# RMSNorm with SiLU: blocks of 512 rows with four rows per partition, and an order fixed by the program

## The chip, the cores and the metric

The kernel runs on one core of a Trainium2 chip. The metric is the device time of one execution in microseconds (us), and the kernel before is given by the median of three runs. One further execution was taken under the profiler; its time is given beside its span, which runs from the first to the last instruction that the trace holds.

The engines that do the work are ACT (ScalarE, activation functions), DVE (VectorE, elementwise work), POOL (GpSimd, here small arithmetic on one value per row) and SP (SyncE, which issues the transfers). TensorE isn't used. Transfers between memory (HBM) and the on-chip buffer (SBUF, 128 partitions) run on 16 DMA engines.

## The reference

The input x has 8 x 1024 = 8192 rows of 2048 float32 values, 67.1 MB; the output has the same shape. Each row is divided by its root mean square, scaled by a vector gamma, and passed through SiLU:

```
rms = sqrt(mean(x ** 2, axis=-1, keepdims=True) + eps)      # eps = 1e-5
out = gamma * x / rms
return out * (1 / (1 + exp(-out)))                          # float32
```

Every value is read once and written once, so the kernel moves 134 MB. A row needs all of its values for its mean before any of them can be scaled.

## The kernel before

The 8192 rows are cut into 64 tiles of 128 rows, one row per partition, so that a tile is 1 MB and each partition holds one run of 8 KB. A pool of 23 buffers (`BUFS`) holds the tiles. Every tile is worked on in place: it is loaded into a buffer, changed there, and stored from the same buffer.

Four functions make up the work on tile i:

- `load(i)` (line 41) issues the transfer of 1 MB from SP.
- `stats(i)` runs Square on ACT (line 59), with the sum of the squares of each row as a second output `ss`; the squares themselves go to a scratch tile `sq` that nobody reads. ACT's accumulator is fetched by a small instruction of its own, which the profile lists as ACTIVATION_READ_ACCUMULATOR. Then POOL computes `var = ss / 2048 + eps` (line 61) and `rstd = var ** -0.5` (line 64), on 128 partitions by one column.
- `scale(i)` multiplies on DVE (line 68): tile times `rstd` of the row times `g`, where `g` is gamma copied to all partitions by POOL at the start (line 47).
- `finish(i)` runs Silu on ACT (line 73), issues the store from SP (line 74), and then issues the load of tile i + 16 (`LEAD`).

The loop at the end calls `stats(i)`, `scale(i - 1)` and `finish(i - 2)`. That is the order of the text, and it isn't the order in which the engines work: the Tile framework takes the program as a set of instructions with dependencies, puts them into an order of its own for each engine, with its own estimate of their times, and adds the semaphores. The order that results is seen only in the timeline. ACT has two kinds of work for each tile, Square and Silu, and works its instructions off in the order in which they were put. Each engine is a queue in this sense: an instruction that waits holds up all that stand behind it.

All transfers are issued from SP and go through one queue (q1 in the profile), which works them off in their order.

Of the kernel before, what the change touches and what calls it, by code (L numbers as in the profile page):

```python
# [1 line left out]

# [4 lines left out]

ACT = mybir.ActivationFunctionType
ALU = mybir.AluOpType


@with_exitstack
def kernel(
    ctx: ExitStack,
    tc: tile.TileContext,
    x: bass.AP,
    gamma: bass.AP,
    eps: bass.AP,
    out: bass.AP,
):  # L20


    nc = tc.nc
    P = nc.NUM_PARTITIONS
    bf16 = mybir.dt.bfloat16
    f32 = mybir.dt.float32
    x2 = x.flatten_outer_dims()
    o2 = out.flatten_outer_dims()
    n, d = x2.shape
    ntiles = n // P  # L30
    BUFS, LEAD = 23, 16

    singles = ctx.enter_context(tc.tile_pool(name="singles", bufs=1))
    pool = ctx.enter_context(tc.tile_pool(name="pool", bufs=BUFS))
    small = ctx.enter_context(tc.tile_pool(name="small", bufs=8))

    xts = {}

    def load(i):
        xt = pool.tile([P, d], f32, name="xt")  # L40
        nc.sync.dma_start(out=xt, in_=x2[i * P:(i + 1) * P])
        xts[i] = xt

    grow = singles.tile([1, d], f32)
    nc.sync.dma_start(out=grow, in_=bass.AP(tensor=gamma.tensor, offset=gamma.offset, ap=[[d, 1], gamma.ap[0]]))
    g = singles.tile([P, d], f32)
    nc.gpsimd.partition_broadcast(g, grow)  # L47
    half = singles.tile([P, 1], f32)
    nc.gpsimd.memset(half, -0.5)  # L49
    sq = singles.tile([P, d], bf16)  # L50

    for i in range(LEAD):
        load(i)

    rstds = {}

    def stats(i):
        ss = small.tile([P, 1], f32, name="ss")
        nc.scalar.activation(out=sq, in_=xts[i], func=ACT.Square, accum_out=ss)  # L59
        var = small.tile([P, 1], f32, name="var")  # L60
        nc.gpsimd.tensor_scalar(out=var, in0=ss, scalar1=1.0 / d, scalar2=float(eps),  # L61
                                op0=ALU.mult, op1=ALU.add)
        rstd = small.tile([P, 1], f32, name="rstd")
        nc.gpsimd.tensor_tensor(out=rstd, in0=var, in1=half, op=ALU.pow)  # L64
        rstds[i] = rstd

    def scale(i):
        nc.vector.scalar_tensor_tensor(out=xts[i], in0=xts[i], scalar=rstds.pop(i), in1=g,  # L68
                                       op0=ALU.mult, op1=ALU.mult)

    def finish(i):
        xt = xts.pop(i)
        nc.scalar.activation(out=xt, in_=xt, func=ACT.Silu)  # L73
        nc.sync.dma_start(out=o2[i * P:(i + 1) * P], in_=xt)
        if i + LEAD < ntiles:
            load(i + LEAD)

    for i in range(ntiles + 2):
        if i < ntiles:
            stats(i)  # L80
        if 0 <= i - 1 < ntiles:
            scale(i - 1)
        if i >= 2:
            finish(i - 2)


# [1 line left out]
_INS = ['x', 'gamma', 'eps']  # L88
_OUTS = [((8, 1024, 2048), 'float32')]

_NUMBERS = {'eps': 9.999999747378752e-06}


# [26 lines left out]
```

## Time and profile before

| | |
|---|---|
| time, median of 3 runs | 413.59 us (413.02 to 413.94) |
| time of the profiled execution | 412.76 us |
| span of the profiled execution | 410.8 us |
| ACT busy | 244.6 us (60%) |
| DVE busy | 150.4 us (37%) |
| POOL busy | 60.1 us (15%) |
| moved | 134.28 MB, mean 327 GB/s over the span |

The page shows the span in 40 slices of 10.27 us; each digit is the busy share of a slice in tenths, so 9 means 90% or more. The row of a group reads: line, engine, operation, output <- inputs, shapes, count | busy us, mean ns of one | idle time of the engine just before these instructions and who ended that idle time. Idle time of an engine that doesn't set the end costs nothing. A row of the timeline reads: start, duration, engine, line, operation, count, and in brackets how long the engine had been idle before and what released it. A row of stretches gives, for each stretch, its length, the busy time and count of DVE, ACT and POOL, the clock, the busy share of the DMA engines and the rate in GB/s.

### The profile page before, as it was taken

What the parts mean: (1) busy time and instruction counts of PE and PEld (TensorE: products, weight loads), DVE (VectorE), ACT (ScalarE), POOL (GpSimd) and SP (SyncE); (2) the same over time, 40 slices, a digit from 0 to 9 for tenths busy, and PEclk for the clock granted to TensorE, in tenths of its full rate; (3) what the DMA queues carried; (4) which work ended last, traced back from release to release, by engine and by line L of the source; (5) the groups of instructions that cost most, each with busy time, mean ns of one, the idle gap of its engine ahead of it and who ended that gap; (6) DMA issues with size and microseconds to landing.
All of it is one profiled execution on the core that took longest, in us unless ns stands there. A gap on an engine that the chain in (4) does not pass through costs nothing.

```text
span 410.8 us, 895 instructions
## 1 busy us (share of the span) xinstructions
DVE 150.4 (37%) x64; ACT 244.6 (60%) x194; POOL 60.1 (15%) x134
## 2 busy tenths in 40 slices
DVE  0067666634242323324424233232424233242422
ACT  4549999984636465554763645556463645546462
POOL 1176212210010101010201010101001010101100
DMA  7999999999999999999999987887844242424334
GB/s 308 419 424 422 416 426 427 425 428 426 427 428 427 428 426 428 427 428 428 428 427 428 365 303 298 300 312 281 295 179 165 112 194 102 204 102 166 140 136 171
DMA packets 18440, 134.28 MB, mean 327 GB/s; under 512 B 2049, under 2 KB 2049, under 8 KB 2049
## 3 DMA queue, kind: packets, MB, share of 16 engines
q1 hardware_dynamic: 18434, 134.23, 80.0%
q14 instruction: 6, 0.05, 0.0%
HBM read 67.12 MB, written 67.11 MB: 327 GB/s over the span
## 4 chain that ended last, share of the span: by engine, by line
issue 76%; POOL 10%; DVE 1%; ACT 0%; POOLq 0%
POOL rstd L64 7%; POOL var L61 3%; DVE xt L68 1%; ACT xt L73 0%; POOLq L64 0%; POOLq L115 0%; ACT sq L59 0%
## 5 line engine op out<-in xcount | busy, mean ns | idle before, releaser
L68 DVE SCALAR_TENSOR_TENSOR xt<-xt,rstd,g 128x2048 f32<-128x2048 f32 x64 | 150.4, 2352 | 253.7 <-POOL rstd L64 252.9
L73 ACT ACTIVATE xt<-xt 128x2048 f32<-128x2048 f32 x64 | 121.7, 1905 | 155.1 <-DVE xt L68 154.0
L59 ACT ACTIVATE sq<-xt 128x2048 bf16<-128x2048 f32 x64 | 121.2, 1894 | 5.7 <-DMA xt<-in_x_dram 5.6
L61 POOL TENSOR_SCALAR var<-ss 128x1 f32<-128x1 f32 x64 | 20.4, 319 | 327.6 <-ACT sq L59 316.1
L64 POOL TENSOR_TENSOR rstd<-var,half 128x1 f32<-128x1 f32 x64 | 37.0, 579 | 5.4 <-POOL var L61 0.2
L59 ACT ACTIVATION_READ_ACCUMULATOR sq<-xt 128x1 f32 x64 | 11.9, 186 | 0.0
L47 POOL PARTITION_BROADCAST g<-grow x1 | 2.3, 2302 | 8.2 <-issue 8.2
L59 ACT ACT_TABLE_LOAD x1 | 1.3, 1283 | 0.7 <-PEq L101 0.7
L73 ACT ACT_TABLE_LOAD x1 | 1.3, 1283 | 0.0
L49 POOL MEMSET half<- 128x1 f32 x1 | 0.1, 99 | 0.3 <-POOLq L101 0.3
L101 POOL MEMSET const-float32-0.0<- 128x1 f32 x1 | 0.1, 98 | 0.2 <-issue 0.2
L101 POOL MEMSET const-bfloat16-1.0<- 128x1 bf16 x1 | 0.1, 101 | 0.0
L101 POOL MEMSET const-uint8-127<- 128x1 uint8 x1 | 0.1, 101 | 0.0
L101 POOL MEMSET const-float32-1.0<- 128x1 f32 x1 | 0.1, 99 | 0.0
## 6 DMA issues: line engine op xcount, KB each, us to landing
xt<-in_x_dram SPq DMA_DIRECT2D x64, 1024.0 KB, 19.6
out_dram<-xt SPq DMA_DIRECT2D x64, 1024.0 KB, 18.2
grow<-in_gamma_dram SPq DMA_DIRECT2D x1, 8.0 KB
```

Of the source, the lines that this page charges most:

```text
L47: nc.gpsimd.partition_broadcast(g, grow)
L49: nc.gpsimd.memset(half, -0.5)
L59: nc.scalar.activation(out=sq, in_=xts[i], func=ACT.Square, accum_out=ss)
L61: nc.gpsimd.tensor_scalar(out=var, in0=ss, scalar1=1.0 / d, scalar2=float(eps), op0=ALU.mult, op1=ALU.add)
L64: nc.gpsimd.tensor_tensor(out=rstd, in0=var, in1=half, op=ALU.pow)
L68: nc.vector.scalar_tensor_tensor(out=xts[i], in0=xts[i], scalar=rstds.pop(i), in1=g, op0=ALU.mult, op1=ALU.mult)
L73: nc.scalar.activation(out=xt, in_=xt, func=ACT.Silu)
L101: nc = _bacc.Bacc("TRN2", target_bir_lowering=False, num_devices=1)
```

## The change

The rows are cut into 16 blocks of 512 rows. Partition p of a block holds four consecutive rows (`J = 4`), which are one run of 32 KB in memory, so that a transfer is 4 MB. Six buffers of 32 KB per partition take the place of 23 of 8 KB, with four blocks loaded at the start (`LEAD = 4`). The first buffer taken from the pool holds gamma until POOL has copied it to all partitions.

The work on a row stays, with these differences:

- Of the four rows of a partition, three are squared and summed on ACT as before; the fourth is done on DVE by `tensor_tensor_reduce`, which multiplies the row by itself and sums. The unused squares go to two float32 tiles in PSUM, `junk_a` for ACT and `junk_v` for DVE, in place of the bf16 tile in SBUF.
- `ss`, `var` and `rstd` have four columns, so POOL runs two instructions per block of 512 rows.
- The multiply on DVE stays one row per partition at a time (four per block). Silu runs on two rows of each partition at once, 4096 elements, after the second and after the fourth multiply.
- The block is stored by one transfer, and the load of block b + 4 is issued after it.
- The body stands in `tc.manual_schedule()`: each engine gets its instructions in the order of the text. That order is `stats(b + 1)` ahead of `finish(b)`, so the Squares of the next block stand ahead of the Silus of this one on ACT, and the reduce of the next block ahead of the multiplies of this one on DVE.

```diff
-    ntiles = n // P
-    BUFS, LEAD = 23, 16
+    J = 4
+    BUFS, LEAD = 6, 4
+    nblk = n // (P * J)
+    xb = x2.rearrange("(b p j) d -> b p (j d)", p=P, j=J)
+    ob = o2.rearrange("(b p j) d -> b p (j d)", p=P, j=J)
...
-    small = ctx.enter_context(tc.tile_pool(name="small", bufs=8))
+    small = ctx.enter_context(tc.tile_pool(name="small", bufs=4))
+    psum = ctx.enter_context(tc.tile_pool(name="psum", bufs=1, space=bass.MemoryType.PSUM))
...
+    junk_a = psum.tile([P, d], f32, name="junk_a")
+    junk_v = psum.tile([P, d], f32, name="junk_v")
...
+    def load(b):
+        xt = pool.tile([P, J * d], f32, name="xt")
+        nc.sync.dma_start(out=xt, in_=xb[b])
+        blocks[b] = xt
...
+    def row(b, j):
+        return blocks[b][:, j * d:(j + 1) * d]
...
+    def stats(b):
+        ss = small.tile([P, J], f32, name="ss")
+        for j in range(J):
+            if j == J - 1:
+                nc.vector.tensor_tensor_reduce(
+                    out=junk_v, in0=row(b, j), in1=row(b, j), scale=1.0, scalar=0.0,
+                    op0=ALU.mult, op1=ALU.add, accum_out=ss[:, j:j + 1])
+            else:
+                nc.scalar.activation(out=junk_a, in_=row(b, j), func=ACT.Square,
+                                     accum_out=ss[:, j:j + 1])
+        var = small.tile([P, J], f32, name="var")
         nc.gpsimd.tensor_scalar(out=var, in0=ss, scalar1=1.0 / d, scalar2=float(eps),
                                 op0=ALU.mult, op1=ALU.add)
+        rstd = small.tile([P, J], f32, name="rstd")
         nc.gpsimd.tensor_tensor(out=rstd, in0=var, in1=half, op=ALU.pow)
+        rstds[b] = rstd
...
+    def finish(b):
+        for j in range(J):
+            nc.vector.scalar_tensor_tensor(out=row(b, j), in0=row(b, j), scalar=rstds[b][:, j:j + 1],
+                                           in1=g, op0=ALU.mult, op1=ALU.mult)
+            if j % 2:
+                pair = blocks[b][:, (j - 1) * d:(j + 1) * d]
+                nc.scalar.activation(out=pair, in_=pair, func=ACT.Silu)
+        nc.sync.dma_start(out=ob[b], in_=blocks.pop(b))
+        del rstds[b]
...
+    with tc.manual_schedule():
+        grow = pool.tile([P, J * d], f32, name="xt")
+        nc.sync.dma_start(out=grow[0:1, 0:d],
+                          in_=bass.AP(tensor=gamma.tensor, offset=gamma.offset, ap=[[d, 1], gamma.ap[0]]))
+        for b in range(LEAD):
+            load(b)
+        nc.gpsimd.memset(half, -0.5)
+        nc.gpsimd.partition_broadcast(g, grow[0:1, 0:d])
+        stats(0)
+        for b in range(nblk):
+            if b + 1 < nblk:
+                stats(b + 1)
+            finish(b)
+            if b + LEAD < nblk:
+                load(b + LEAD)
```

More of the change, by code (lines that the diff above doesn't have):

```diff
@@ L24 @@
     P = nc.NUM_PARTITIONS
-    bf16 = mybir.dt.bfloat16
     f32 = mybir.dt.float32
@@ L29 @@
     n, d = x2.shape
-    ntiles = n // P
-    BUFS, LEAD = 23, 16
+    J = 4
[3 more added lines that the diff above has]
+    ob = o2.rearrange("(b p j) d -> b p (j d)", p=P, j=J)
     singles = ctx.enter_context(tc.tile_pool(name="singles", bufs=1))
     pool = ctx.enter_context(tc.tile_pool(name="pool", bufs=BUFS))
-    small = ctx.enter_context(tc.tile_pool(name="small", bufs=8))
[L37 to L42, printed above, removed]
@@ L44 @@
-    grow = singles.tile([1, d], f32)
-    nc.sync.dma_start(out=grow, in_=bass.AP(tensor=gamma.tensor, offset=gamma.offset, ap=[[d, 1], gamma.ap[0]]))
-    g = singles.tile([P, d], f32)
[L47 to L60, printed above, removed]
+    small = ctx.enter_context(tc.tile_pool(name="small", bufs=4))
@@ new lines @@
+    psum = ctx.enter_context(tc.tile_pool(name="psum", bufs=1, space=bass.MemoryType.PSUM))
+    g = singles.tile([P, d], f32)
+    half = singles.tile([P, J], f32)
+    junk_a = psum.tile([P, d], f32, name="junk_a")
+    junk_v = psum.tile([P, d], f32, name="junk_v")
+    blocks, rstds = {}, {}
+    def load(b):
[4 more added lines that the diff above has]
+        return blocks[b][:, j * d:(j + 1) * d]
@@ L61, in stats @@
         nc.gpsimd.tensor_scalar(out=var, in0=ss, scalar1=1.0 / d, scalar2=float(eps),
                                 op0=ALU.mult, op1=ALU.add)
-        rstd = small.tile([P, 1], f32, name="rstd")
+        rstd = small.tile([P, J], f32, name="rstd")
         nc.gpsimd.tensor_tensor(out=rstd, in0=var, in1=half, op=ALU.pow)
[L65 to L84, printed above, removed]
+        rstds[b] = rstd
[8 more added lines that the diff above has]
+        del rstds[b]
```

## The prediction

> **What bounds the kernel now.** I read the page's busy times and slices first, then the groups, the timeline, the waits, and the stretches at both ends.
>
> ```profile
> span 410.8 us, 895 instructions
> DVE 150.4 (37%) x64; ACT 244.6 (60%) x194; POOL 60.1 (15%) x134
> ...
> DMA  7999999999999999999999987887844242424334
> GB/s 308 419 424 422 416 426 427 425 428 426 427 428 427 428 426 428 427 428 428 428 427 428 365 303 298 300 312 281 295 179 165 112 194 102 204 102 166 140 136 171
> ...
> q1 hardware_dynamic: 18434, 134.23, 80.0%
> ...
> HBM read 67.12 MB, written 67.11 MB: 327 GB/s over the span
> ```
>
> No engine is busy for more than 60% of the span, and the DMA runs full for 22 of 40 slices (some 226 us) and then falls to a third. So the transfers do not set the end, and neither does any engine's total work: an order does. The groups give the durations, the timeline the order:
>
> ```profile
> L68 DVE SCALAR_TENSOR_TENSOR xt<-xt,rstd,g 128x2048 f32<-128x2048 f32 x64 | 150.4, 2352 | 253.7 <-POOL rstd L64 252.9 <-DMA xt<-in_x_dram 0.8
> L73 ACT ACTIVATE xt<-xt 128x2048 f32<-128x2048 f32 x64 | 121.7, 1905 | 155.1 <-DVE xt L68 154.0 <-DMA out_dram<-xt 1.2
> L59 ACT ACTIVATE sq<-xt 128x2048 bf16<-128x2048 f32 x64 | 121.2, 1894 | 5.7 <-DMA xt<-in_x_dram 5.6
> L64 POOL TENSOR_TENSOR rstd<-var,half 128x1 f32<-128x1 f32 x64 | 37.0, 579 | 5.4 <-POOL var L61 0.2
> L61 POOL TENSOR_SCALAR var<-ss 128x1 f32<-128x1 f32 x64 | 20.4, 319 | 327.6 <-ACT sq L59 316.1 <-issue 11.2
> L59 ACT ACTIVATION_READ_ACCUMULATOR sq<-xt 128x1 f32 x64 | 11.9, 186 | 0.0
> ```
>
> ```profile
> 22.52 0.45 POOL L61 TENSOR_SCALAR var<-ss 128x1 f32<-128x1 f32 x2 [11.22 <-issue]
> ...
> 83.74 5.49 ACT L73 ACTIVATE xt<-xt 128x2048 f32<-128x2048 f32 x3
> ...
> 401.24 0.55 POOL L64 TENSOR_TENSOR rstd<-var,half 128x1 f32<-128x1 f32 x1
> 401.82 2.35 DVE L68 SCALAR_TENSOR_TENSOR xt<-xt,rstd,g 128x2048 f32<-128x2048 f32 x1 [4.78 <-POOL rstd L64]
> 404.20 1.91 ACT L73 ACTIVATE xt<-xt 128x2048 f32<-128x2048 f32 x1 [3.33 <-DVE xt L68]
> 406.14 0.33 SPq L74 DMA_DIRECT2D out_dram<-xt  x1
> ...
> 379.57 0.19 POOL L61 TENSOR_SCALAR var<-ss 128x1 f32<-128x1 f32 x1 [6.31 <-ACT sq L59]
> ...
> 386.70 0.19 POOL L61 TENSOR_SCALAR var<-ss 128x1 f32<-128x1 f32 x1 [6.31 <-ACT sq L59]
> ```
>
> At 83.74 us ACT runs three Silus in a row and has none in stock afterwards. From there ACT does Silu of a tile, Square of the next, and then waits 3.33 us: the next Silu needs the DVE multiply, which needs POOL's rstd, which needs that same Square. POOL's row returns every 7.13 us (379.57 to 386.70). That loop, 7.13 us a tile from about 84 us to the last Silu (some 45 tiles, 321 us), sets the end. The tiles themselves are there early: the Squares waited 5.6 us in all for loads. The transfers' own floor comes from a stretch in which they ran without a gap, loads and stores mixed:
>
> ```profile
> DMA packets 7031, 51.24 MB, mean 427 GB/s; under 512 B 777, under 2 KB 777, under 8 KB 777
> ```
>
> At 427 GB/s (60 to 180 us) the 134.28 MB would need 314.5 us.
>
> **The change part by part.**
>
> *Order.* In the new text ACT gets, per block of 512 rows, three Squares of the next block and two double Silus of this one; DVE one reduce of the next block, then four multiplies of this one. The multiplies of block b need only the statistics of b, finished a whole block earlier, so the loop goes. ACT per block: 3 x 1.90 us (Square and its accumulator read, which overlap slightly; the rows give 1.894 and 0.186) plus 2 x 3.66 us (5.49 us for three Silus, so 1.83 each) = 13.0 us. DVE: 4 x 2.352 = 9.4 us plus the reduce.
>
> *The reduce*, tensor_tensor_reduce, is in no row. Its bounds: 2.35 us (the multiply, also two inputs of 2048 elements in one pass) and 4.7 us (twice that, as for two passes). I take 2.35, the nearest row. DVE then has 11.8 us a block, at worst 14.1. *The double Silu* is bounded by 3.6 and 3.8 us (1.83 and 1.905 us twice); the Squares' target in PSUM I leave at 1.894 us. *POOL* gets tiles of four columns: 0.19 and 0.55 us at one column as the timeline has them, at most four times that (3.0 us), 16 times instead of 64. All of this lies under the transfers, because a block's load and store, 8.39 MB, take 19.6 us at 427 GB/s. Without that cover ACT would be the limit, 16 x 13.0 = 208 us, still less.
>
> *Transfers.* The bytes stay. 128 transfers of 1 MB become 32 of 4 MB, and runs of 8 KB become 32 KB; no row has such a size. To bound it:
>
> ```profile
> 1.00:3.00 2.00, 0.00 (x0) 1.00 (x1) 0.00 (x0) 1.00 0.37 66
> 3.00:6.10 3.10, 0.00 (x0) 0.01 (x1) 0.00 (x0) 1.00 0.97 402
> 6.10:42.00 35.90, 15.01 (x7) 24.86 (x21) 16.78 (x15) 1.00 1.01 422
> 406.10:407.00 0.90, 0.00 (x0) 0.01 (x1) 0.00 (x0) 1.00 0.15 64
> 407.00:409.40 2.40, 0.00 (x0) 0.00 (x0) 0.00 (x0) 1.00 1.00 413
> 409.40:410.80 1.40, 0.00 (x0) 0.00 (x0) 0.00 (x0) 1.00 0.01 0
> ...
> 236.00:300.00 64.00, 21.17 (x9) 34.05 (x28) 6.64 (x18) 1.00 0.82 294
> ```
>
> (columns after the stretch: its length, DVE, ACT, POOL, clock, DMA share, GB/s). A store alone on idle queues moved at 413 GB/s and 1 MB transfers in a full queue at 427: what belongs to a transfer rather than to its bytes is visible at some 3%. A quarter as many transfers and runs could save three quarters of as much again, 2.4%, so 437 GB/s at best; at worst the large runs do no better than the lone store, 413. I take 432, the middle of 427 and 437, since each engine still has eight runs and one small completion packet per transfer, but each run is four times as long: 134.28 / 0.432 = 310.8 us.
>
> The Trainium skill (DMA: Bandwidth & Descriptors, Where 436 GB/s comes from) puts the ceiling at 435.2 GB/s, 16 ports of 32 B at 850 MHz. As an estimate from that page the transfers would take 308.5 us, 2.3 less than my term; the 427 of this trace lies below the ceiling, as it must.
>
> *Queueing on SP.* One queue still carries gamma, four loads, then store b and load b+4 in turn. A load of block b+4 sits behind the store of b, which waits for the last double Silu of b. It also needs the buffer of b-2, whose store is two block times older. Before, eight transfers were in flight:
>
> ```profile
> xt<-in_x_dram SPq DMA_DIRECT2D x24, 1024.0 KB, 19.6
> ...
> SPq L74 <- ACT xt L73: 203.4, 34, 6.7
> SPq L41 <- DMA xt<-in_x_dram: 80.0, 40, 2.7
> SPq L74 <- DMA out_dram<-xt: 61.1, 29, 2.1
> ```
>
> 19.6 us to landing is eight times 2.45 us, and SP waited for older transfers 141 us in all. If that limit counts transfers, eight of 4 MB never bind; if bytes, two still bridge 19.4 us of queue. So SP's waits cost nothing as long as each store is issued before the queue runs dry. That I work out at the two ends, where least stands ahead of it.
>
> *Head.* First bytes by the rows above: by 6.1 us 1.38 MB had moved (2 x 66 + 3.1 x 402 kB), 3.3 us worth at 422, so the start costs 2.8 us. A block takes 9.7 us. Block 1 lands at 2.8 + 19.4 + 0.5 = 22.7; the reduce ends at 25.1 (POOL's first arithmetic came at 22.5 before, and is in time); four multiplies to 34.5, the last double Silu to 38.1, and 0.9 us more to the first byte of the store (406.14 to 407.0): 39.0. The four loads occupy the queue until 2.8 + 38.8 = 41.6. So there is 2.6 us of slack, 0.2 with the slow reduce.
>
> *Tail.* Load 15 is the 28th block to move and lands at 2.8 + 28 x 9.7 = 274.4, say 275. Stores 12 and 13 then still fill the queue until 294.4. Store 14 waits for the reduce of 15 and the multiplies of 14: 275 + 2.35 + 9.4 + 3.66 + 0.9 = 291.3. Store 15: 9.4 us later, 300.7, against 304.1. Slack 3.1 and 3.4 us, about 1 with the slow reduce. So I put the gaps at 0, at most 3 us.
>
> *Sum.* 2.8 start + 310.8 transfers + 0.5 (the four unmixed loads at 422 rather than 427) + 0.6 (four unmixed stores at the end, between 0 and the 1.3 us that 413 would cost) + 1.3 after the last byte (the last stretch above) = 316.0 us of span. The profiled execution took 412.76 us at a span of 410.8, so 2.0 us lie around it: 318.0. The median of the runs lay 0.8 above the profiled one, so 319.
>
> **The rivals.**
>
> *Turn-taking inside a block.* If a multiply on one row waits for the Silu on another row of the same buffer, DVE pauses 3.66 us between its second and third multiply. A block then takes DVE 15.4 us (19.1 if it pauses after the fourth too), still under 19.4; but head and tail lose their slack, 1.1 + 0.6 + 2.7 us: about 323. For it: one buffer now holds what four did. Against: the text addresses each row by its own columns.
>
> *The pinned order does not decouple.* If each block's statistics are waited for in its own turn, as now, a block costs 5.7 + 0.74 + 9.4 + 3.66 = 19.5 us, and 21.9 with the reduce in line; with 12.8 us until the first block lands and 11.9 us for the last store that is 337 to 375 of span, so 340 to 378. For it: that is exactly what the timeline shows now. Against: Squares of b+1 stand ahead of the Silus of b in the new text.
>
> *Slower: the large strides collide in memory.* Sixteen engines would walk addresses four times as far apart as now. If that costs transfer rate everywhere, the kernel is slower from 134.28 MB / (412.8 - 2.0 - 2.8 - 1.3 us) = 330 GB/s downwards. At the lowest sustained rate of a busy stretch here, 294 GB/s (236 to 300 us), it would take 456.7 + 6.1 = 463 us. Against it: a block stays one contiguous 4 MB piece, and the full slices hold 426 to 428 GB/s whatever addresses they pass; the 294 comes with stores issued one by one, not with full queues.
>
> For that rival the Trainium skill has a rule (the same page, Latency and other measured facts): row pitches at large powers of two slow copies, 207 GB/s each way at 512 KiB and 164 at 2 MiB against 214. Here the pitch goes from 8 to 32 KiB, below all of these, so by that rule little is lost; no run so far shows it.
>
> **How the numbers follow.** The forecast, transfers bound from end to end, gets 0.77; turn-taking 0.10; no decoupling 0.08; collision 0.05, of which 0.04 ends slower than before and 0.01 level. Low end: 437 GB/s without gaps, 307.3 + 4.6 + 2.8 = 314.7. High end: 413 GB/s with 3 us of gaps, 325.1 + 4.1 + 3 + 2.8 = 335. I give 313 to 336, which holds the forecast and turn-taking. The last two rivals lie outside. What a measurement of this kernel can tell from no change is about 0.2%: faster 0.95, same 0.01, slower 0.04.
>
> **What would show it.** Right: DMA slices at 9 from the second to the last, near 432 GB/s; POOL's 7.13 us loop gone; the Squares, not the Silus, waiting longest, and for loads; SP's stores no longer behind ACT after the head. DVE busy about 188 us (80 passes at 2.35), ACT about 205. Reduce wrong: its row above 4.7 us. Turn-taking: multiplies released by Silu. No decoupling: multiplies again released by POOL with long waits, and a DMA share below 9. Collision: a share at 9 with GB/s well under 413. Store gaps at the ends would show as single low slices after the fourth and before the last.

## The result and the profile after

The changed kernel takes 322.24 us (median of 4 runs, 321.28 to 323.22), against 413.3 us for the kernel before, timed beside it: a ratio of 0.7796, 95% interval 0.7766 to 0.7825. The forecast was 319 us with a range of 313 to 336. The profiled execution took 322.79 us at a span of 321.0.

From the page of the changed kernel, the busy times, the slices, the queue and the groups:

```profile
span 321.0 us, 432 instructions
DVE 181.7 (57%) x96; ACT 213.8 (67%) x130; POOL 59.5 (19%) x38
...
DMA  8999999999999999999999999999999999997994
GB/s 315 404 441 437 416 408 437 421 412 457 416 421 449 422 433 429 421 449 430 425 441 416 437 445 408 437 437 429 437 433 425 449 412 437 445 404 314 457 416 204
...
q1 hardware_dynamic: 4610, 134.23, 97.7%
...
L74 DVE SCALAR_TENSOR_TENSOR xt<-xt,rstd,g 128x2048 f32<-128x2048 f32 x64 | 146.1, 2347 | 1.1 <-POOL rstd L69 1.1
L63 ACT ACTIVATE junk_a<-xt 128x2048 f32<-128x2048 f32 x48 | 90.3, 1881 | 67.8 <-DMA xt<-in_x_dram 66.8
L78 ACT ACTIVATE xt<-xt 128x4096 f32<-128x4096 f32 x32 | 115.5, 3616 | 22.9 <-DVE xt L74 22.9
L59 DVE CUSTOM_DVE_ANT_0 junk_v<-xt 128x2048 f32<-128x2048 f32 x16 | 36.8, 2300 | 118.8 <-DMA xt<-in_x_dram 118.8
...
xt<-in_x_dram SPq DMA_DIRECT2D x16, 4096.0 KB, 43.0
out_dram<-xt SPq DMA_DIRECT2D x16, 4096.0 KB, 33.7
```

The DMA was full for 22 of 40 slices and is full for nearly all of them now. The multiplies on DVE, which used to wait 252.9 us in all for POOL's rstd, wait 1.1 us. What the engines wait for is the loads: 118.8 us on DVE ahead of the reduce, 66.8 us on ACT ahead of the Squares. That is the picture of a kernel bound by its transfers. From issue to landing a transfer takes 34 to 43 us (the medians), so each is issued with about three others of 9.7 us still ahead of it.

One sign that the prediction named did not come: SP's stores still stand behind ACT, all sixteen of them.

```profile
SPq L79 <- ACT xt L78: 276.0, 16, 25.4
```

(Waits of SP: total us, times, longest.) In the middle of the span that wait costs nothing, because about three transfers still stand in the queue while SP waits; a wait of the engine that issues says little about the queue behind it.

The stretches of the changed kernel (columns as in the prediction):

```profile
60.00:260.00 200.00, 113.53 (x60) 137.25 (x82) 37.54 (x21) 1.00 1.00 431
...
290.00:300.00 10.00, 10.00 (x6) 8.18 (x3) 1.16 (x1) 1.00 0.82 351
...
316.00:321.00 5.00, 0.00 (x0) 0.00 (x0) 0.00 (x0) 1.00 0.12 52
```

431 GB/s in the middle, a dip at 290 to 300 us, and a tail in which an eighth of the DMA capacity is still at work.

### The profile page after: what moved, and what is told of

Same layout as the page of the kernel before. It is cut to its first block, busy times and chain, and to the rows that moved or that the text cites. A ratio compares the mean times of both kernels' runs of the same rounds, so it can differ in the third digit from the quotient of the medians.

```text
span 321.0 us, 432 instructions
## 1 busy us (share of the span) xinstructions
DVE 181.7 (57%) x96; ACT 213.8 (67%) x130; POOL 59.5 (19%) x38
## 2 busy tenths in 40 slices
DMA packets 4612, 134.24 MB, mean 418 GB/s; under 512 B 513, under 2 KB 513, under 8 KB 513
## 4 chain that ended last, share of the span: by engine, by line
DMA 60%; DVE 17%; ACT 13%; issue 5%; DVEq 1%; SPq 1%; ACTq 0%
DMA xt<-in_x_dram 60%; DVE xt L74 16%; ACT xt L78 8%; ACT junk_a L63 4%; DVEq L127 1%; SPq L79 0%; DVE ss L59 0%; DVE junk_v L59 0%; SPq L49 0%; SPq L84 0%; DVEq L59 0%; ACTq L63 0%; DVEq L74 0%
## 5 line engine op out<-in xcount | busy, mean ns | idle before, releaser
L74 DVE SCALAR_TENSOR_TENSOR xt<-xt,rstd,g 128x2048 f32<-128x2048 f32 x64 | 146.1, 2347 | 1.1 <-POOL rstd L69 1.1
L63 ACT ACTIVATE junk_a<-xt 128x2048 f32<-128x2048 f32 x48 | 90.3, 1881 | 67.8 <-DMA xt<-in_x_dram 66.8
L78 ACT ACTIVATE xt<-xt 128x4096 f32<-128x4096 f32 x32 | 115.5, 3616 | 22.9 <-DVE xt L74 22.9
L59 DVE CUSTOM_DVE_ANT_0 junk_v<-xt 128x2048 f32<-128x2048 f32 x16 | 36.8, 2300 | 118.8 <-DMA xt<-in_x_dram 118.8
L66 POOL TENSOR_SCALAR var<-ss 128x4 f32<-128x4 f32 x16 | 14.9, 931 | 221.6 <-ACT junk_a L63 210.5
L69 POOL TENSOR_TENSOR rstd<-var,half 128x4 f32<-128x4 f32 x16 | 42.0, 2624 | 1.3
L63 ACT ACTIVATION_READ_ACCUMULATOR junk_a<-xt 128x1 f32 x48 | 9.0, 187 | 0.0
L89 POOL PARTITION_BROADCAST g<-xt x1 | 2.3, 2303 | 8.2 <-issue 8.2
L59 DVE DVE_READ_ACCUMULATOR2_ANT ss<- 128x1 f32 x16 | 2.3, 142 | 0.0
```

The lines of the kernel that those rows point to most:

```text
L59: nc.vector.tensor_tensor_reduce(out=junk_v, in0=row(b, j), in1=row(b, j), scale=1.0, scalar=0.0, op0=ALU.mult, op1=ALU.add, accum_out=ss[ ...
L63: nc.scalar.activation(out=junk_a, in_=row(b, j), func=ACT.Square, accum_out=ss[:, j:j + 1])
L74: nc.vector.scalar_tensor_tensor(out=row(b, j), in0=row(b, j), scalar=rstds[b][:, j:j + 1], in1=g, op0=ALU.mult, op1=ALU.mult)
L78: nc.scalar.activation(out=pair, in_=pair, func=ACT.Silu)
L89: nc.gpsimd.partition_broadcast(g, grow[0:1, 0:d])
```

## The experiments

### Which part of the change is the gain: the order or the blocks

The first kernel is the one before with its own text order pinned and nothing else: tiles of 128 rows, 23 buffers, 1 MB transfers. What is left out in the diff are the load of gamma, its broadcast and the 16 first loads, which move into the block.

```diff
+    with tc.manual_schedule():
...
         for i in range(ntiles + 2):
             if i < ntiles:
                 stats(i)
             if 0 <= i - 1 < ntiles:
                 scale(i - 1)
             if i >= 2:
                 finish(i - 2)
```

> The kernel before (tiles of 128 rows, 1 MB transfers, 23 buffers, Square of every row on ACT) with one edit: its own text order is pinned on every engine. Theory (the order is the gain, the size of the blocks next to nothing): the 7.13 us loop goes, ACT needs 3.7 us a tile against 4.9 us of transfers, and the time is that of 134.28 MB at 427 GB/s, 314.5 + 2.8 + 1.3 of span, 319 to 323 us. Rival (the large blocks carry the gain): well above 340 us. Rival (4 MB transfers are worth some 2% of rate): 4 to 6 us above the changed kernel, so 326 to 328.

It takes 323.03 us (322.81 to 323.18; ratio 0.7822, 0.781 to 0.7834). Its page and its stretch of 60 to 260 us:

```profile
span 321.3 us, 895 instructions
DVE 150.5 (47%) x64; ACT 242.3 (75%) x194; POOL 58.7 (18%) x134
...
DMA  7999999999999999999999999999999999999995
```

```profile
DMA packets 11731, 85.43 MB, mean 427 GB/s; under 512 B 1303, under 2 KB 1303, under 8 KB 1303
```

In the middle of its timeline ACT has no wait for DVE any more:

```profile
183.27 1.91 ACT L53 ACTIVATE sq<-xt 128x2048 bf16<-128x2048 f32 x1 [1.10 <-DMA xt<-in_x_dram]
...
185.18 1.89 ACT L67 ACTIVATE xt<-xt 128x2048 f32<-128x2048 f32 x1
...
188.18 1.91 ACT L53 ACTIVATE sq<-xt 128x2048 bf16<-128x2048 f32 x1 [1.10 <-DMA xt<-in_x_dram]
```

The Silu follows the Square at once, and what ACT waits for is the next load; a tile takes 4.91 us, which is its 2.1 MB at 427 GB/s. The same instruction count as the kernel before, 895, and the time of the changed kernel. The order alone carries the whole gain that can be measured: the two intervals overlap. The rival of 326 to 328 us for the small transfers is out too, though the mean rate is indeed lower, 427 against 431 GB/s.

The second kernel is the opposite: blocks of 512 rows, reduce and double Silu, without the pinned order.

```diff
-    with tc.manual_schedule():
+    if True:
```

> The changed kernel without the pinned order: blocks of 512 rows, order left to the framework, which puts Square and Silu of one block next to each other on ACT from the fourth block on. Theory (order is the gain): a block then costs 6.1 (Squares) + 3.7 (POOL on four columns) + 9.2 (four multiplies) + 3.6 (last Silu) = 22.6 us against 19.4 us of transfers, so about 13.5 + 16 x 22.6 - 25 (first blocks overlap) + 12 = 350 to 375 us. Rival (the blocks are the gain): 322 us as the changed kernel.

It takes 336.72 us (336.24 to 338.04; ratio 0.8159, 0.8138 to 0.8181). Its timeline in the middle:

```profile
181.12 0.34 SPq L79 DMA_DIRECT2D out_dram<-xt  x1
...
187.13 0.19 POOL L66 TENSOR_SCALAR var<-ss 128x4 f32<-128x4 f32 x1 [18.87 <-ACT junk_a L63]
187.41 1.01 POOL L69 TENSOR_TENSOR rstd<-var,half 128x4 f32<-128x4 f32 x1
188.45 9.14 DVE L74 SCALAR_TENSOR_TENSOR xt<-xt,rstd,g 128x2048 f32<-128x2048 f32 x4 [8.74 <-POOL rstd L69]
193.10 3.62 ACT L78 ACTIVATE xt<-xt 128x4096 f32<-128x4096 f32 x1 [6.05 <-DVE xt L74]
...
201.26 0.34 SPq L79 DMA_DIRECT2D out_dram<-xt  x1
```

The loop of the kernel before is back: DVE waits 8.74 us for POOL, POOL 18.87 us for the Squares. But one turn now serves 512 rows and takes 20.14 us (181.12 to 201.26), where four turns of 7.13 us were needed before, 28.5 us. So the blocks are a second, weaker cure for the same wait: they dilute it to just over the 19.4 us of transfers. The 350 to 375 us expected were too high above all by the price of POOL: 3.7 us a block had been taken, and it is 0.19 + 1.01 here, while DVE stands still (more on that below). That is 40 us over sixteen blocks; the same sum with 20.14 us a block gives 323 us of span, and 334.5 were measured, so the 25 us taken off for the overlap of the first blocks was too much by some 12.

This is also what the prediction's rival without decoupling describes: 19.5 us a block had been reckoned for it, and the time measured here lies a little below the 340 us at which that rival began.

### What bounds the changed kernel

Its transfers alone; of `finish(b)` only the store is left:

```diff
-        stats(0)
         for b in range(nblk):
-            if b + 1 < nblk:
-                stats(b + 1)
             finish(b)
```

> The changed kernel's transfers alone: the same 4 MB loads and stores in the same buffers, no arithmetic at all, so that the output is the input. Theory (transfers set the end): within 3 us of the changed kernel, 319 to 323 us; four of sixteen DMA queues finish each transfer late, growing to some 6 us, also without any engine working, since the lag belongs to the transfers. Rival (the late queues come from the engines' work on the same memory): no lag, and 315 to 317 us.

321.43 us (320.78 to 321.69; ratio 0.7781, 0.7768 to 0.7795), the time of the whole kernel within a quarter of a per cent. All of the arithmetic is covered: the transfers set the end. The rival of 315 to 317 us, in which the work of the engines slows the transfers, is out.

Next, whether the share between ACT and DVE matters: all four Squares on ACT and no reduce on DVE.

```diff
-            if j == J - 1:
-                nc.vector.tensor_tensor_reduce(...)
-            else:
-                nc.scalar.activation(out=junk_a, in_=row(b, j), func=ACT.Square, ...)
+            nc.scalar.activation(out=junk_a, in_=row(b, j), func=ACT.Square, ...)
```

> The changed kernel with all four Squares of a block on ACT, no reduce on DVE. Theory (compute is covered): ACT needs 15.2 us a block against 19.4 us of transfers, and DVE 9.2; the time stays within 1 us of the changed kernel, 321 to 323 us. Rival (the share between ACT and DVE matters): two more us per block, up to 350 us.

322.62 us (321.89 to 323.61; ratio 0.7821, 0.7797 to 0.7844): no difference. The reduce on DVE buys nothing here. The groups of this kernel and the POOL rows of the changed kernel's page show something else:

```profile
L63 POOL TENSOR_TENSOR rstd<-var,half 128x4 f32<-128x4 f32 x16 | 16.2, 1011 | 1.3
...
L60 POOL TENSOR_SCALAR var<-ss 128x4 f32<-128x4 f32 x16 | 3.8, 237 | 257.3 <-ACT junk_a L57 257.3
```

```profile
L66 POOL TENSOR_SCALAR var<-ss 128x4 f32<-128x4 f32 x16 | 14.9, 931 | 221.6 <-ACT junk_a L63 210.5
L69 POOL TENSOR_TENSOR rstd<-var,half 128x4 f32<-128x4 f32 x16 | 42.0, 2624 | 1.3
```

The same two POOL instructions take 0.24 and 1.01 us where DVE waits for them, and 0.93 and 2.62 us on average in the changed kernel, where DVE is mostly multiplying the block before. Within the changed kernel it is the same: rstd takes 1.01 us at 48.82 us, with DVE idle, and 2.99 us at 249.31 us, beside the multiplies.

### How much stands ahead of each store

The prediction worked out that a store is issued just before the queue would run dry. Fewer blocks loaded ahead, three in one kernel and two in another, take that stock away, with the same six buffers:

```diff
-    BUFS, LEAD = 6, 4
+    BUFS, LEAD = 6, 3
```

> The changed kernel with three blocks loaded at the start. Theory (same arithmetic of the queue): the queue runs dry once at the head, from 31.9 us to the first store's first byte at 39.8, 7.9 us; in between each store is issued some 3 us before it is needed; at the tail store 14 comes some 6 us late; 322 + 8 to 14 us, so 330 to 337 us. Rival (the lead has slack to spare): 322 to 324 us. Rival (the slack of 3 us a block isn't there in fact): more than 340 us.

> The changed kernel with two blocks loaded at the start instead of four (six buffers as before). Theory (the queue hides the compute only while two transfers stand ahead of each store): a block then costs its landing, 15.2 us until its predecessor's store can be issued (reduce 2.4, four multiplies 9.2, last double Silu 3.6), 0.9 to the first byte and 19.4 of transfers, 35.8 us; 59.6 + 13 x 35.8 + 15.2 + 0.9 + 19.4 = 560 us of span, 550 to 570 us. Rival (the order alone decides, the lead doesn't matter): 322 us.

With three: 338.18 us (337.64 to 340.52; ratio 0.8197, 0.8159 to 0.8235). With two: 580.65 us (580.53 and 580.78; ratio 1.4054, 1.4022 to 1.4086), slower than the kernel before. Stretches of the kernel with three, then the stores of the kernel with two:

```profile
31.00:41.00 10.00, 10.00 (x6) 9.52 (x6) 2.72 (x1) 1.00 0.30 125
41.00:300.00 259.00, 141.94 (x76) 169.96 (x103) 47.55 (x26) 1.00 1.00 424
300.00:310.00 10.00, 10.00 (x6) 9.12 (x7) 3.74 (x2) 1.00 0.57 246
310.00:320.00 10.00, 10.00 (x5) 7.39 (x3) 0.00 (x0) 1.00 0.49 210
```

```profile
223.95 0.34 SPq L79 DMA_DIRECT2D out_dram<-xt  x1
...
260.92 0.34 SPq L79 DMA_DIRECT2D out_dram<-xt  x1
```

With three the queue runs dry exactly where the arithmetic put it: at the head, 31 to 41 us at a share of 0.30 (7 us lost), and at the tail, 300 to 320 us at 0.57 and 0.49 (9 us lost, where 6 had been reckoned, which puts the time 1 us above the range). With two, each block costs 36.97 us where 35.8 had been reckoned, 15 us over thirteen blocks, and the time is 580.65 instead of 550 to 570: compute and transfers take turns. So the pinned order needs its lead: three blocks keep the queue full in the middle (424 GB/s at a share of 1.00) but not at the ends, four cover the ends too, and two cover nothing.

### The dip at 295 us, and the late engines

The prediction expected the transfers to end at 2.8 + 310.8 + about 1 us; the last completion mark comes at 319.8 us, some 5 us later, although the mean rate in the middle is the one expected. The trace has a completion mark of each of the sixteen DMA engines for each transfer, and they aren't together. In the changed kernel twelve engines finish most transfers within some 0.5 us of each other; four are late, by more and more as the run goes on. The table gives the largest time from the first to the last engine's mark of one transfer, from the marks in each trace, and the mean rate from the stretches:

```
kernel                                      largest spread   rate 60 to 260 us
changed kernel                              6.3 us           431 GB/s
kernel before, order pinned (1 MB)          3.2 us           427
transfers alone                             4.9 us           430
four Squares on ACT                         3.4 us           428
stores of 2 MB, below                       6.4 us           430
runs of 8 KB, below                         3.3 us           426
loads alone, below                          0.5 us           431
stores alone, below (45 to 195 us)          1.4 us           433
transfers in twos, below                    3.4 us           426
```

The dip came under suspicion first. In the timeline of the changed kernel the last double Silu of block 14 is this one:

```profile
292.59 3.62 ACT L78 ACTIVATE xt<-xt 128x4096 f32<-128x4096 f32 x1 [0.91 <-DVE xt L74]
```

It ends at 296.2 us, and only then is store 14 issued; by their marks the twelve engines had finished store 13 at 294.2 to 295.7, the last of the late ones at 300.5. So the twelve run dry and the late ones don't. Storing each half block as soon as its Silu is done closes the dip:

```diff
             if j % 2:
                 pair = blocks[b][:, (j - 1) * d:(j + 1) * d]
                 nc.scalar.activation(out=pair, in_=pair, func=ACT.Silu)
+                nc.sync.dma_start(out=ob[b][:, (j - 1) * d:(j + 1) * d], in_=pair)
-        nc.sync.dma_start(out=ob[b], in_=blocks.pop(b))
+        blocks.pop(b)
```

> The changed kernel with each block stored in two transfers of 2 MB, one behind each double Silu, so that the stores of the last two blocks start some 4.5 us earlier. Theory (the dip in the DMA share near 295 us costs nothing, since the four late engines never run dry and end the span): unchanged, 321 to 324 us, and the dip goes. Rival (the dip, some 2.5 us on twelve engines, is on the path): 319 to 320 us.

323.57 us (323.42 to 323.99; ratio 0.7835, 0.7824 to 0.7845): not faster. Its stretches:

```profile
290.00:300.00 10.00, 10.00 (x5) 8.18 (x3) 2.19 (x1) 1.00 1.01 434
...
310.00:316.00 6.00, 0.00 (x0) 0.00 (x0) 0.00 (x0) 1.00 0.78 336
316.00:321.00 5.00, 0.00 (x0) 0.00 (x0) 0.00 (x0) 1.00 0.18 79
```

The dip is gone (1.01), and the time saved by the twelve engines reappears as a tail in which only the late ones work: the twelve finish the last store at 314.6 to 315.8 us instead of 317, the late ones at 319.8 to 321.0 instead of 319.5 to 319.8. The dip was free; the late engines end the span.

Does a second queue fill their pauses? Stores issued from ACT:

```diff
-        nc.sync.dma_start(out=ob[b], in_=blocks.pop(b))
+        nc.scalar.dma_start(out=ob[b], in_=blocks.pop(b))
```

> The changed kernel with its stores issued from ACT, right behind the last Silu of a block, on a queue of their own; loads stay on SP. Theory (each of the sixteen DMA engines is full already, 432 GB/s on twelve, some 424 on the late four): no change, 320 to 324 us, late engines as before. Rival (one queue in order is what makes four engines late, a second queue fills their pauses): all engines at 432 GB/s, 316 to 318 us.

Its six runs scatter from 319.07 to 331.16 us around a median of 326.42, where the runs of every other kernel lie within 3 us of each other. One run lies below all runs of the changed kernel, one among them and four above, so no steady gain is shown, and the rival's 316 to 318 is out. In its trace, taken of the run at 327.40 us, the spread reaches 12.9 us; why its runs scatter stays open. The Trainium skill (DMA: Bandwidth & Descriptors, Issuing engines are not separate DMA queues) says that transfers issued from several engines run on the same sixteen DMA engines and that this saves only issue time; that no steady gain came agrees with it.

Is it the length of the runs? The same 4 MB transfers with rows dealt out 128 apart, four runs of 8 KB per partition:

```diff
-    xb = x2.rearrange("(b p j) d -> b p (j d)", p=P, j=J)
-    ob = o2.rearrange("(b p j) d -> b p (j d)", p=P, j=J)
+    xb = x2.rearrange("(b j p) d -> b p j d", p=P, j=J)
+    ob = o2.rearrange("(b j p) d -> b p j d", p=P, j=J)
...
-        nc.sync.dma_start(out=xt, in_=xb[b])
+        nc.sync.dma_start(out=xt.rearrange("p (j d) -> p j d", j=J), in_=xb[b])
...
-        nc.sync.dma_start(out=ob[b], in_=blocks.pop(b))
+        nc.sync.dma_start(out=ob[b], in_=blocks.pop(b).rearrange("p (j d) -> p j d", j=J))
```

> The changed kernel with the rows of a block dealt out as in the kernel before: transfers stay 4 MB, but each partition holds four rows that lie 128 rows apart, so that the runs are 8 KB instead of 32 KB. Theory (run length sets the rate of the engines that are on time, the late ones set the end): the mean rate between 60 and 260 us falls from 431 to about 427 GB/s, the time moves by less than 1%, 321 to 325 us. Rival (transfer size sets the rate): 431 GB/s as in the changed kernel. Rival (runs set the time): 325 to 327 us.

323.82 us (323.51 to 323.91; ratio 0.7838, 0.7828 to 0.7848). Its stretch of 60 to 260 us:

```profile
60.00:260.00 200.00, 113.53 (x60) 137.48 (x82) 39.39 (x21) 1.00 1.01 426
```

8 KB runs give 426 in 4 MB transfers as they gave 427 in 1 MB ones, 32 KB runs 431. The mean rate alone would not prove that the run decides, since kernels with 32 KB runs lie between 426 and 431 in the table. The durations of the single packets in the traces do (a packet is one run of one partition, moved by one engine): a packet of 8 KB takes 309 ns (the median) in this kernel and in the pinned kernel of 1 MB transfers, so 32 KB take 1236 ns; a packet of 32 KB takes 1213. So the run sets the rate of an engine, and the transfer doesn't. On the time this is worth 0.5% (323.82 against 322.24), less than the 1.2% between the mean rates; the smaller spread with the short runs fits that.

What makes engines late? Loads alone, every block twice, and then, in a kernel of its own, four loads and then stores alone. Both leave out all of the arithmetic; the first leaves out all stores but one.

```diff
-        for b in range(LEAD):
+        for b in range(nblk):
+            load(b)
+        for b in range(nblk):
             load(b)
...
+        nc.sync.dma_start(out=ob[nblk - 1], in_=blocks[nblk - 1])
```

```diff
-        stats(0)
         for b in range(nblk):
-            if b + 1 < nblk:
-                stats(b + 1)
-            finish(b)
-            if b + LEAD < nblk:
-                load(b + LEAD)
+            nc.sync.dma_start(out=ob[b], in_=blocks[b % LEAD])
```

> Loads alone: every block loaded twice, 32 loads of 4 MB in the changed kernel's shape, no arithmetic, and one store of the last block at the end; all other output is left out. Theory (lateness belongs to DMA engines under reads as well): four engines fall behind, 134 MB of reads plus one store of 4 MB take about 330 us. Rival (lateness comes from reads and writes mixed): no lag, 432 GB/s on all engines, 325 us.

> Four loads of 4 MB and then sixteen stores of 4 MB from the same four buffers, no arithmetic; the output holds the first four blocks over and over. Loads alone had shown all sixteen engines within 0.5 us of each other. Theory (stores make engines late): the spread between the first and the last engine of a store grows to some 2 to 4 us over the sixteen, and the rate lies below 432, so 200 to 204 us. Rival (only loads and stores mixed make them late): the spread stays at 0.5 us and the stores run at 432 GB/s, 198 to 199 us.

328.13 us for 138.4 MB, of which the last 4 MB, the store, wait for the last load; and 201.64 us (one run) for 83.9 MB:

```profile
60.00:260.00 200.00, 0.00 (x0) 1.00 1.00 431
```

```profile
45.00:195.00 150.00, 0.00 (x0) 1.00 1.00 433
```

Both went against the theory that stood at the time. Loads alone keep all sixteen engines within 0.5 us for the whole run, and stores alone within 1.4 us without growth; the expectation of a lag under loads, and then of a lag under stores, fell one after the other. The 32 loads, as many bytes as the whole kernel moves, have landed at 314.3 us, where the changed kernel needs until 319.8. Late engines of this kind are seen only where the two kinds are mixed, and even there not at once: with the transfers alone but mixed, all sixteen stay within 0.8 us until 112 us. (The 201.64 us lies in the range of the fallen theory; the spread, which it was about, doesn't.)

If it is the change between the kinds, fewer changes should help. Two stores, then two loads:

```diff
             finish(b)
-            if b + LEAD < nblk:
-                load(b + LEAD)
+            if b % 2:
+                for c in (b + LEAD - 1, b + LEAD):
+                    if c < nblk:
+                        load(c)
```

> The changed kernel with its transfers grouped in twos: stores of blocks b and b+1, then the loads of b+4 and b+5, so that the queue changes between reading and writing half as often. Loads alone and stores alone had kept all engines within 0.5 and 1.3 us at 431 to 433 GB/s; only the mixed runs had late engines. Theory (the change between the two kinds costs the late engines): spread at the end halves from 6.3 to about 3 us, 318.5 to 321 us. Rival (it is the mix itself, however it is cut): spread of 5 to 7 us, 322 to 324 us. Rival (the longer wait for a load takes the slack of the queue): dips in the DMA share, 325 to 335 us.

323.74 us (322.68 to 324.66; ratio 0.783, 0.7811 to 0.7849). The spread falls to 3.4 us, about what the theory said, and the time doesn't move. Stretches of this kernel:

```profile
30.00:60.00 30.00, 27.92 (x15) 29.43 (x18) 10.59 (x6) 1.00 0.98 405
...
290.00:310.00 20.00, 14.14 (x7) 17.57 (x8) 2.62 (x2) 1.00 0.94 406
```

The loads now wait for a second store, and the queue runs thin at both ends (405 and 406 GB/s), so on-time engines idle and late ones catch up. The two effects aren't separated by this run.

The packets show where the time goes, if not why. In the changed kernel a 32 KB packet takes 1.213 us in the median. Of the 4096, 88 that start after the first 4 us take over 5% longer, up to 2.2 us, and together 33 us more; four engines late by 6.3 us each make 25, which fits. 76 of the 88 lie within some 3 us of one of the 13 places where the queue goes from a load to a store, 2 near one of the 12 where it goes from a store to a load. Loads alone have one long packet after the first 4 us; stores alone have 26, all at 39 to 42 us, where their loads end and the stores begin. So in the changed kernel most of the cost sits at the change from load to store. The transfers in twos have fewer such changes, 7 instead of 13, and yet more long packets, 180 that cost 90 us together: a small spread isn't a small loss, and this run doesn't bear out that fewer changes cost less. Why a packet gets long at such a change stays open.

## Why the prediction was right

The diagnosis held and was the whole of it: the 7.13 us loop that ACT's order made, and not the transfers, set the end before, and with the order alone pinned the time falls to 323.0 us. The floor named for it, 314.5 us at 427 GB/s plus the ends, comes to 320.6 us with the start, the end and what lies around the span, and every version with a pinned order and a lead of four, on one queue, landed within 4 us above it (the pinned kernel with its lead of sixteen tiles, the same 16 MB, counts here).

By the steps:

- *Order.* DVE's multiplies come four in a row without waiting for Silu or POOL:

```profile
26.08 9.14 DVE L74 SCALAR_TENSOR_TENSOR xt<-xt,rstd,g 128x2048 f32<-128x2048 f32 x4
...
31.20 3.62 ACT L78 ACTIVATE xt<-xt 128x4096 f32<-128x4096 f32 x1
...
38.90 0.35 SPq L79 DMA_DIRECT2D out_dram<-xt  x1
...
281.18 1.88 ACT L63 ACTIVATE junk_a<-xt 128x2048 f32<-128x2048 f32 x1 [4.36 <-DMA xt<-in_x_dram]
...
283.42 18.19 DVE L74 SCALAR_TENSOR_TENSOR xt<-xt,rstd,g 128x2048 f32<-128x2048 f32 x8
```

  The Silu on the first two rows runs from 31.20 to 34.82 us, beside the third and fourth multiply. That refutes turn-taking inside a block, although its 323 us lie nearer to the measured 322.24 than the forecast does: the number alone would have picked the wrong mechanism. The absent wait for POOL refutes the rival without decoupling.
- *The reduce*: 2.35 us taken, 2.300 measured, with an accumulator read behind it. The double Silu: 3.66 taken, 3.616 measured. DVE 181.7 us busy against 188, ACT 213.8 against 205.
- *POOL*: at most 3.0 us taken for the two instructions, 0.93 + 2.62 = 3.55 measured. The bound was broken, because its rows came from moments when DVE stood still; the means of the groups, 0.319 and 0.579, would have given 3.6. It cost nothing: the result is needed a block later.
- *Transfers*: 432 GB/s taken, 431 measured from 60 to 260 us. The middle between 427 and 437 was a guess, and it hit by luck: 32 KB in 1.213 us on sixteen engines are 432 GB/s. But the term of 310.8 us was mis-sized all the same, since it took one rate for sixteen engines and nothing for the changes between loads and stores. The late ones ended some 5 us later than that rate says, and the span came out at 321.0 instead of 316.0. With the last completion mark 1.2 us ahead of the end, the whole ran at 134.24 MB / (319.8 - 2.8 us) = 423 GB/s.
- *Around the span*: 2.0 us taken, 1.8 measured; and the median, put 0.8 us above the profiled execution, lay 0.6 below it. By that luck a span 5.0 us too short became a time only 3.2 us too short.
- *Head*: store 0 was to be issued at 38.1 us and was at 38.90.
- *Tail*: load 15 was to land at 275 us. The twelve engines finished it at 274.8 to 276.4, the last of the late ones at 281.1, and ACT started at 281.18. Store 14 left a dip of about 2 us for the twelve engines, within the 0 to 3 us allowed; closing it gained nothing.
- *Collision of large strides*: nothing of the kind. 32 KB runs are the faster ones: 431 GB/s against 426 with 8 KB runs.

The parts of the change that the prediction priced as covered are covered indeed: the transfers alone take 321.4 us. Of the title's three parts, the order was the gain; the large blocks and runs were worth 0.5% at most, beside it, and the six buffers with a lead of four are what the order needs at that size.

## What to carry to other kernels

When no engine and no queue is busy all the time, look for two adjacent rows of the timeline whose spacing repeats to the hundredth of a microsecond, and ask which instruction stands in front of which on that engine; writing the order down cost nothing here and was worth 22%. Before making transfers larger, run them alone: if the time of the copy is the time of the kernel, as here after the change, what is left lies in the transfers and their queue and not in the arithmetic. And count in transfers what stands ahead of each store when it is issued: taking one block away from the lead cost 16 us, taking two made the kernel slower than it was.

## What the runs showed that had not been expected

- Some DMA engines fall behind when loads and stores of 4 MB share a queue: up to 6.3 us by the 30th of 32 transfers in the changed kernel, against 0.5 us for loads alone and 1.4 us for stores alone. They end the span while the other twelve are done. The packets that take too long lie at the changes from a load to a store: 76 of 88 in the changed kernel, only one in loads alone.
- A packet of 8 KB takes 309 ns in transfers of 1 MB and of 4 MB alike, and one of 32 KB takes 1213, so four short ones take 1.9% longer than one long one.
- POOL's small instructions slow down while DVE multiplies two SBUF operands: 1.01 to 2.62 us for rstd on four columns, 0.24 to 0.93 us for var. The Trainium skill (SBUF — State Buffer, Who interferes with whom) says that a DVE instruction with two SBUF inputs takes a read interface that it shares with GpSimd; these rows agree.
